# Last projection of a hybrid encoder: weight sums and norm products moved from GpSimd to VectorE

## The chip, the core and the metric

The kernel runs on one core of a Trainium2 chip. A core has TensorE (matrix multiplies, "PE" in the profile, with its weight loads listed apart as "PEld"), VectorE ("DVE"), ScalarE ("ACT"), GpSimd ("POOL"), and SyncE ("SP"), whose queue issues the DMA transfers of this kernel. The engines run side by side, each through its own list of instructions in a fixed order, and wait for each other by semaphores. Matrix multiplies read their operands from the on-chip memory SBUF and add into banks of PSUM; main memory is reached by DMA only. The metric is the device time of one execution in microseconds (us), median of several runs.

## The reference: what is computed

One encoder layer on 1280 tokens (1024 of a prompt, 256 of a sample) with 2048 channels. After an RMS norm and an input projection, eight heads of neighbourhood attention and four heads of a bidirectional mLSTM are computed, gated and put side by side into `mixed`, 2048 channels again. The last step, which this change concerns, is

```python
    mixed = jnp.concatenate([att, mem], axis=-1)
    return x + jnp.einsum('btm,md->btd', mixed, w_out)
# and around it
    x = hybrid_layer(...)
    return rmsnorm(x, final_norm_w)
```

that is, a product of 1280 x 2048 by 2048 x 2048 in fp32, the residual `x`, and a norm over each token's 2048 outputs, multiplied by `final_norm_w`.

## The kernel before

The input projection, the attention and the mLSTM come first and fill the first 2220 us. They are not touched. Their last part, the late gates, runs into the beginning of the last projection.

**The last projection with seven products.** The 2048 output columns are done in two halves, `p = 0` and `p = 1`, of two blocks of 512 columns each (`n0 = 2p`, `n1 = 2p + 1`). `mixed` is cut into four blocks: the tokens in two halves of 640, the 2048 inputs in two halves of 1024. With the weights cut in the same way (B11, B12 the blocks of the first 1024 inputs, B21, B22 those of the last 1024, the second index being the column block), one column half is a 2 x 2 by 2 x 2 block product, and it is done with seven block products in place of eight. `product(p, i, ...)` does the one named `i`, and `operands(p, i, kk)` returns its two operands for one block `kk` of 128 inputs (eight of them). The lists `Aa`, `Ac`, `Ad`, `Ae` hold the blocks of `mixed` in SBUF; `e` is overwritten on the way with sums. The weight operands are

- `i == 2`: B21; `i == 1`: B11; `i == 3`: B22, loaded in pairs of `kk` by `w_pure`;
- `i == 5`: B12 - B11; `i == 6`: `T2`, which is B22 - (B12 - B11); `i == 7`: B22 - B12; `i == 4`: `T2` - B21.

These weight sums are made on chip from blocks of 128 x 512 that `w_block` loads into the buffer pool `po` (six buffers, shared, in turn, by all of them), and, for `T2`, into a slot that held a part of the input `x` before (`xslot`). The order of the products is 2, 5, 1, 6, 7, 4, 3 in the first half and 5, 1, 6, 7, 4, 3, 2 in the second.

**A block of a product.** Both operands are split in two fp32r parts, a rounded one and the rest: `split` (lines 150 to 152) has ScalarE cast (line 151) and VectorE subtract (line 152). The tiles are `mo` (128 x 640, of `mixed`) and `wo` (128 x 512, of the weights), four buffers each. Then TensorE does 15 matmuls of 128x128 by 128x512 (line 1300): three for each of the five token tiles `tt`, into five PSUM banks. The last two blocks of a product are held (`HOLD = 2`) and done bank by bank, so that the banks end one after the other. Then `y_add` (line 1250, VectorE) adds each bank to the output tiles `Y` that it belongs to; where it belongs to two, there are two additions. `Y` starts as the residual, by DMA (`y_init`, line 1257).

**The end of an output tile.** When a tile has got all its additions, `y_done` sums its squares with ScalarE (line 1263), multiplies it with `final_norm_w` (`fnb`) on GpSimd (line 1265) for 30 of the 40 tiles, and stores the tiles of `p = 0` to `yD` in main memory. `finish` reads them back, scales a token's four tiles by the reciprocal root (`rs`, lines 1280 to 1289, two tiny GpSimd instructions each) and stores the result.

**On GpSimd** stand, per block and column half, four weight sums: line 1227 (B12 - B11) and line 1228 (`T2`), both at product 5, line 1241 at product 7 and line 1245 at product 4; and the 30 norm products of line 1265. Other sums of `mixed` blocks (lines 1214, 1231, 1237) are on VectorE.

**Order.** No order is written out by hand here: a scheduler in the compiler orders each engine's instructions by its own estimate of their times, so a change in one place moves others. All DMA transfers of this part are issued from SP's queue, one after the other; a transfer that waits for a buffer holds up those behind it.

Of the kernel before, what the change touches and what calls it, by code (L numbers as in the profile page):

```python
# [11 lines left out]
ALU = mybir.AluOpType  # L12
# [26 lines left out]
def kernel(  # L39
# [17 lines left out]
    V, S, G, PE, DM = nc.vector, nc.scalar, nc.gpsimd, nc.tensor, nc.sync  # L57
# [408 lines left out]
    def po(name):  # L466
        return wb.tile([P, 520], F32, tag="po", name=name, bufs=NPO)

    def w_piece(src, name):
        raw = wb.tile([P, 1024], F32, tag="wraw", name=f"wr_{name}", bufs=2)  # L470
        dst = raw
        if len(src.shape) == 3:
            dst = raw.rearrange("p (j c) -> p j c", j=2)
        DM.dma_start(dst, src)
        return raw
# [699 lines left out]
    def xslot(i, name, dt=F32):  # L1175
        pool, tag = XTAGS[i]
        return pool.tile([P, GB], dt, tag=tag, name=name)
# [10 lines left out]
    fnb = [xslot(28 + i, f"fnb{i}") for i in range(4)]  # L1188
    T2 = {}
    Y = {}  # L1190
# [4 lines left out]
    def w_block(kh, nb, kk, name):  # L1195
        raw = po(f"wb_{name}")[:, :512]
        DM.dma_start(raw, w_o[nb, :, (8 * kh + kk) * 512 : (8 * kh + kk + 1) * 512])
        return raw

    def w_pure(kh, nb, kk, name):  # L1200
        k = 8 * kh + kk
        if kk % 2 == 0:
            src = w_o[nb, :, k * 512 : (k + 2) * 512]
            pair_of["n"] = pair_of.get("n", -1) + 1
            if pair_of["n"] % 3 == 2:
                pair_of["w"] = mp.tile([P, 1024], F32, tag="wr2", name=f"wp_{name}")
                DM.dma_start(pair_of["w"], src)
            else:
                pair_of["w"] = w_piece(src, f"wp_{name}")
        return pair_of["w"][:, (kk % 2) * 512 : (kk % 2 + 1) * 512]  # L1210

    def m_sum(x, y_, op, name):
        t = mp.tile([P, TH], F32, tag="ms", name=name, bufs=2)
        V.tensor_tensor(t, x, y_, op=op)  # L1214
        return t

    def operands(p, i, kk):
        nm = f"{p}_{i}_{kk}"
        n0, n1 = 2 * p, 2 * p + 1
        a, c, d, e = Aa[kk], Ac[kk], Ad[kk], Ae[kk]  # L1220
        if i == 2:
            return d, w_pure(1, n0, kk, nm)
        if i == 5:
            b12, b11 = w_block(0, n1, kk, nm + "a"), w_block(0, n0, kk, nm + "b")
            t = T2[kk] = xslot(20 + kk, f"T2_{nm}")
            DM.dma_start(t, w_o[n1, :, (8 + kk) * 512 : (9 + kk) * 512])
            G.tensor_tensor(b12, b12, b11, op=ALU.subtract)  # L1227
            G.tensor_tensor(t, t, b12, op=ALU.subtract)
            if p:
                return m_sum(e, a, ALU.add, f"ms{nm}"), b12  # L1230
            V.tensor_tensor(e, e, c, op=ALU.add)
            return e, b12
        if i == 1:
            return a, w_pure(0, n0, kk, nm)
        if i == 6:
            if p == 0:
                V.tensor_tensor(e, e, a, op=ALU.subtract)  # L1237
            return e, T2[kk]
        if i == 7:
            b22, b12 = w_block(1, n1, kk, nm + "a"), w_block(0, n1, kk, nm + "b")  # L1240
            G.tensor_tensor(b22, b22, b12, op=ALU.subtract)
            return m_sum(c, e, ALU.subtract, f"ms{nm}"), b22
        if i == 4:
            b21 = w_block(1, n0, kk, nm)
            G.tensor_tensor(b21, T2[kk], b21, op=ALU.subtract)
            return c, b21
        return m_sum(d, e, ALU.subtract, f"ms{nm}"), w_pure(1, n1, kk, nm)

# [10 lines left out]
    def y_done(p, q, tt):  # L1259
        th, nh = divmod(q, 2)  # L1260
        t, c = th * NT + tt, 2 * p + nh
        jk = mp.tile([P, 512], F32, tag="jk", name=f"jk{p}_{q}_{tt}", bufs=1)
        S.activation(jk, Y[p, q, tt], AF.Square, accum_out=ss[t][:, c : c + 1])  # L1263
        if p == 0 or q in (1, 3):
            G.tensor_tensor(Y[p, q, tt], Y[p, q, tt], fnb[c], op=ALU.mult)  # L1265
        if p == 0:
            DM.dma_start(yD[t][:, nh * 512 : (nh + 1) * 512], Y[p, q, tt])

# [25 lines left out]
    def product(p, i, bk, first, each):  # L1294
# [11 lines left out]
        for kk in range(8):  # L1306
            nm = f"{p}_{i}_{kk}"
            ms, wsrc = operands(p, i, kk)
            if tail:
                m = [  # L1310
                    mp.tile([P, TH], F32R, tag=f"mb{z}{z}{kk}", name=f"mo{nm}_{z}") for z in range(2)
                ]
            else:
                t = mp.tile([P, 2, TH], F32R, tag="mo", name=f"mo{nm}", bufs=4)
                m = [t[:, z] for z in range(2)]
            split(*m, ms)
            if tail and kk >= 4:
                w = [xslot(2 * kk + 12 + z, f"wt{nm}_{z}", F32R) for z in range(2)]
            else:
                t = wb.tile([P, 2, 544], F32R, tag="wsp", name=f"wo_{nm}", bufs=4)  # L1320
                w = [t[:, z, :512] for z in range(2)]
            split(*w, wsrc)
            if tail or kk >= 8 - HOLD:
                held.append((kk, m, w))
                continue
            for tt in range(NT):
                mms(tt, kk, m, w, False)
# [13 lines left out]
    for p in range(2):  # L1341

        def reads(bk, *adds, done=None, fin=None):
            def each(tt):
                for q, op in adds:
                    y_add(p, q, tt, bk[tt], op)
                if done is not None:
                    y_done(p, done, tt)
                if fin is not None and p == 1:
                    finish(fin, tt)  # L1350
            return each
# [114 lines left out]
```

## Time and profile before

| | |
|---|---|
| median of 3 runs | 2636.76 us (2635.14 to 2638.74) |
| the profiled execution | 2639.76 us, its span 2637.7 us |
| clock granted to TensorE, mean | 0.996 of full speed |
| first and last weight load of line 1300 | 2222.0 and 2628.1 us |
| GpSimd busy between 2222 and 2629 us | 158.97 us |
| VectorE busy in the same time | 333.56 us |

The profile is of one execution. "Span" runs from its first to its last instruction. A row of a group names the line, the engine, the operation, the tiles written and read, their shapes and the count, then the busy time and the mean length, then the idle time of the engine just before and who ended it (the releaser). Tile names are shortened: `wb_3a` stands for a weight block of `kk = 3`, `T` for `T2`. A row of the time line gives start, length, engine, line, tiles and the number of instructions merged into it. Matmuls overlap, so a row's mean length is longer than the distance between two starts.

### The profile page before, as it was taken

The page shows a single profiled execution, that of the slowest core. Times are in us where ns is not written, and L with a number is a line of the kernel's source. Part 1 is how long each engine was busy: PE and PEld are TensorE (multiplying, and loading weights), DVE is VectorE, ACT ScalarE, POOL GpSimd, SP SyncE. Part 2 cuts the span into 40 slices and gives each one's busy share as a digit, 9 for nine tenths or more (in the row PEclk, how much of TensorE's full clock was granted, in tenths as well). Part 3 has the DMA queues.
Part 4 walks back from the last instruction along what each step waited for, and adds up shares of the span by engine and source line. Part 5 has one row for each costly group of instructions (what it writes and reads, how often), then busy time and mean ns, then how long its engine had stood idle before and what let it go on. Part 6 is the DMA issues. An engine that isn't in the chain of part 4 may idle for free.

```text
span 2637.7 us, 42477 instructions
## 1 busy us (share of the span) xinstructions
PE 2582.4 (98%) x14470; PEld 2364.1 (90%) x14470; DVE 1923.2 (73%) x3744; ACT 1309.2 (50%) x2988; POOL 709.1 (27%) x951
## 2 busy tenths in 40 slices
PE   8999999999999999999999999999999999999998
PEld 8999999999999999988998998989888888787777
DVE  7858778787878778774586587677566644989796
ACT  7534444444444444543565566566566423344435
POOL 0434444444444444300011011010000000436232
PEclk9999999999999999999999999999999999999999
DMA  6423333233333232444655646655554567445327
GB/s 209 150 77 118 107 124 112 95 99 101 95 96 109 77 114 91 163 122 147 193 158 172 198 146 190 201 154 177 186 183 150 178 227 278 158 124 189 103 78 254
DMA packets 215648, 389.10 MB, mean 148 GB/s; under 512 B 26976, under 2 KB 116232, under 8 KB 215432
## 3 DMA queue, kind: packets, MB, share of 16 engines
q1 hardware_dynamic: 215432, 386.40, 46.0%
q8 instruction: 114, 1.87, 0.3%
q14 instruction: 102, 0.84, 0.1%
HBM read 314.94 MB, written 71.38 MB: 146 GB/s over the span
## 4 chain that ended last, share of the span: by engine, by line
PE 45%; DVE 8%; DMA 4%; ACT 2%; issue 1%; SPq 1%; POOL 0%; ACTq 0%; POOLq 0%; DVEq 0%
PE pc L497 21%; PE po L1300 10%; PE pv L578 4%; DVE mo L152 2%; DVE wo L152 1%; PE A54b L188 1%; DMA wr<-in_w_in_dram 1%; DVE ms L1214 1%; PE A52b L188 1%; DVE y L1250 1%; PE nap_0s L615 1%; PE nap_1s L615 1%; DMA nap_0vr<-vD 0%; DVE mb L1237 0%; PE nap_2o L741 0%
## 5 line engine op out<-in xcount | busy, mean ns | idle before, releaser
L1300 PE MATMUL po<-wo,mo 128*128 128x512 f32 x1620 | 381.0, 395 | 12.5 <-DVE wo L152 9.9
L1300 PEld LDWEIGHTS po<-wo,mo 128*128 128x128 f32 x1620 | 303.8, 188 | 88.9 <-DVE wo L152 14.9
L152 DVE TENSOR_TENSOR ws<-wr,ws 128x512 fp32r<-128x512 f32 x224 | 153.3, 695 | 119.3 <-ACT ws L151 118.0
L151 ACT CAST ws<-wr 128x512 fp32r<-128x512 f32 x224 | 136.6, 619 | 179.1 <-PE pc L497 116.8
L151 ACT CAST mo<-mb 128x640 fp32r<-128x640 f32 x72 | 51.8, 725 | 108.1 <-PE po L1300 92.4
L152 DVE TENSOR_TENSOR mo<-mb,mo 128x640 fp32r<-128x640 f32 x72 | 72.9, 1023 | 38.8 <-ACT mo L151 38.8
L1250 DVE TENSOR_TENSOR y<-y,po 128x512 f32<-128x512 f32 x90 | 57.6, 678 | 12.8 <-PE po L1300 12.8
L151 ACT CAST mo<-ms 128x640 fp32r<-128x640 f32 x40 | 29.0, 725 | 70.8 <-PE po L1300 32.5
L102 POOL TENSOR_SCALAR mls_0r<-mls_0r 128x2 f32<-128x2 f32 x4 | 1.2, 289 | 234.0 <-ACT mls_0jk L1087 234.0
L152 DVE TENSOR_TENSOR mo<-ms,mo 128x640 fp32r<-128x640 f32 x40 | 48.5, 1214 | 13.2 <-ACT mo L151 13.2
L1265 POOL TENSOR_TENSOR y<-y,fnb 128x512 f32<-128x512 f32 x30 | 48.1, 1621 | 36.3 <-ACT jk L1263 35.8
L152 DVE TENSOR_TENSOR wsv<-wr_v,wsv 128x512 fp32r<-128x512 f32 x64 | 44.0, 693 | 17.5 <-ACT wsv L151 16.8
L151 ACT CAST wsv<-wr_v 128x512 fp32r<-128x512 f32 x64 | 38.9, 617 | 30.8 <-PE pc L497 19.2
L165 DVE TENSOR_TENSOR pco<-pc,rstdb 128x512 f32<-128x512 f32 x48 | 32.8, 686 | 27.8 <-PE pc L497 26.1
L1227 POOL TENSOR_TENSOR wb_0a<-wb_0a,wb_0b 128x512 f32<-128x512 f32 x2 | 2.6, 1302 | 179.5 <-DMA wb_0b<-in_w_o_dram 179.5
L274 DVE SCALAR_TENSOR_TENSOR pcv<-pco,cw_sb,pcv 128x516 f32<-128x516 f32 x64 | 46.7, 749 | 0.0
L1214 DVE TENSOR_TENSOR ms<-mb,mb 128x640 f32<-128x640 f32 x40 | 45.1, 1127 | 0.0
L1263 ACT ACTIVATE jk<-y 128x512 f32<-128x512 f32 x40 | 25.2, 631 | 39.7 <-DVE y L1250 38.2
L497 PE MATMUL pc<-x_0h,ws 128*128 128x512 f32 x112 | 36.5, 406 | 0.9 <-DVE pco L165 0.9
L497 PE MATMUL pc<-x_2h,ws 128*128 128x512 f32 x112 | 35.3, 399 | 0.0
L188 PE MATMUL fb<-xb,fw 128*128 128x384 f32 x96 | 24.7, 374 | 10.8 <-ACT xb L158 10.8
L188 PE MATMUL fb<-xg,fw 128*128 128x384 f32 x192 | 35.1, 336 | 0.1
(1701 smaller groups left out, 8268.9 us busy)
## 6 DMA issues: line engine op xcount, KB each, us to landing
wr<-in_w_in_dram SPq DMA_DIRECT2D x112, 512.0 KB
wr_v<-in_w_in_dram SPq DMA_DIRECT2D x32, 512.0 KB
xq<-in_xtok_dram SPq DMA_DIRECT2D x20, 512.0 KB
mb<-mx SPq DMA_DIRECT2D x32, 320.0 KB
y<-in_xtok_dram SPq DMA_DIRECT2D x40, 256.0 KB
wr_wp<-in_w_o_dram SPq DMA_DIRECT2D x16, 512.0 KB
xr<-in_xT_dram SPq DMA_DIRECT2D x16, 384.0 KB
nap_0bt<-in_rpb_tab_dram SPq DMA_DIRECT2D x32, 192.0 KB
```

The lines of the kernel that those rows point to most:

```text
L151: S.copy(hi, src)
L152: V.tensor_tensor(lo, src, f(hi), op=ALU.subtract)
L165: V.tensor_tensor(o, src, rb, op=ALU.mult)
L188: PE.matmul(o, w(a_), x(b_), start=first and m == 0, stop=last and m == 2)
L274: V.scalar_tensor_tensor(dst[:, a:n], src[:, a + j - pad : n + j - pad], cw_sb[:, ct, j : j + 1], dst[:, a:n], op0=ALU.mult, op1=ALU.add,)
L497: PE.matmul(pb[j], t[j][:, wi, c : c + P], xs[xi], start=first and m == 0, stop=last and m == 2,)
L578: PE.matmul(outs[tt], xs[:, tt * P : (tt + 1) * P], t[:, wi, q * w : (q + 1) * w], start=first and m == 0 and (gates or tt % 2 == 0), stop ...
L615: PE.matmul(b[:, :nkeys], qs(a_), ks(b_), start=i == 0, stop=i == 2)
L1214: V.tensor_tensor(t, x, y_, op=op)
L1250: V.tensor_tensor(Y[p, q, tt], Y[p, q, tt], bk, op=op)
L1265: G.tensor_tensor(Y[p, q, tt], Y[p, q, tt], fnb[c], op=ALU.mult)
L1300: PE.matmul(bk[tt], m[xi][:, tt * P : (tt + 1) * P], w[wi], start=first and kk == 0 and j == 0, stop=last and j == 2, skip_group_check=True,)
```

## The change

At `i == 5`, B12 is now loaded straight into the slot of `T2` and B11 is subtracted from it there, by VectorE; that tile is product 5's weight operand. At `i == 1`, the next product, B22 is loaded into a `po` buffer and `T2` becomes B22 minus what it held, again by VectorE. The sums of products 7 and 4 and the norm products of `y_done` go from GpSimd (`G`) to VectorE (`V`). The numbers of transfers and matmuls are as before.

```diff
         if i == 5:
-            b12, b11 = w_block(0, n1, kk, nm + "a"), w_block(0, n0, kk, nm + "b")
+            b11 = w_block(0, n0, kk, nm)
             t = T2[kk] = xslot(20 + kk, f"T2_{nm}")
-            DM.dma_start(t, w_o[n1, :, (8 + kk) * 512 : (9 + kk) * 512])
-            G.tensor_tensor(b12, b12, b11, op=ALU.subtract)
-            G.tensor_tensor(t, t, b12, op=ALU.subtract)
+            DM.dma_start(t, w_o[n1, :, kk * 512 : (kk + 1) * 512])
+            V.tensor_tensor(t, t, b11, op=ALU.subtract)
             if p:
-                return m_sum(e, a, ALU.add, f"ms{nm}"), b12
+                return m_sum(e, a, ALU.add, f"ms{nm}"), t
             V.tensor_tensor(e, e, c, op=ALU.add)
-            return e, b12
+            return e, t
         if i == 1:
+            b22 = w_block(1, n1, kk, nm)
+            V.tensor_tensor(T2[kk], b22, T2[kk], op=ALU.subtract)
             return a, w_pure(0, n0, kk, nm)
...
         if i == 7:
             b22, b12 = w_block(1, n1, kk, nm + "a"), w_block(0, n1, kk, nm + "b")
-            G.tensor_tensor(b22, b22, b12, op=ALU.subtract)
+            V.tensor_tensor(b22, b22, b12, op=ALU.subtract)
             return m_sum(c, e, ALU.subtract, f"ms{nm}"), b22
         if i == 4:
             b21 = w_block(1, n0, kk, nm)
-            G.tensor_tensor(b21, T2[kk], b21, op=ALU.subtract)
+            V.tensor_tensor(b21, T2[kk], b21, op=ALU.subtract)
             return c, b21
...
         if p == 0 or q in (1, 3):
-            G.tensor_tensor(Y[p, q, tt], Y[p, q, tt], fnb[c], op=ALU.mult)
+            V.tensor_tensor(Y[p, q, tt], Y[p, q, tt], fnb[c], op=ALU.mult)
```

In the kernel after the change the new sum at `i == 5` is line 1227, that at `i == 1` line 1234, those of products 7 and 4 lines 1242 and 1246, and the norm product line 1266.

## The prediction

> **What bounds the kernel now.** I read the page first, for the whole span, then the time table of stretches for the last projection, then the weight loads of TensorE in order of time, then VectorE and GpSimd beside each other.
>
> ```profile
> span 2637.7 us, 42477 instructions
> PE 2582.4 (98%) x14470; PEld 2364.1 (90%) x14470; DVE 1923.2 (73%) x3744; ACT 1309.2 (50%) x2988; POOL 709.1 (27%) x951
> ```
>
> TensorE is the bound, so the change can only be worth the time in which TensorE stands still in the stage that it touches. That stage is the 1680 matmuls of line 1300; their first and last weight loads:
>
> ```profile
> L1300 PEld LDWEIGHTS po<-wo,mo x1620: 186/188/331, 2222.0 to 2625.4; 128*128 128x128 f32 x180
> L1300 PEld LDWEIGHTS po<-wt,mo x60: 187/188/188, 2607.8 to 2628.1; 128*128 128x128 f32 x60
> ```
>
> From 2222.0 to 2628.3 are 406.3 us. An undisturbed run of the same loads gives the pace (each row: start, length, instructions, idle before it):
>
> ```profile
> 2257.55 3.30 PEld L1300 LDWEIGHTS po<-wo,mo 128*128 128x128 f32 x15 [3.00 <-DVE wo L152]
> ...
> 2292.41 118.12 PEld L1300 LDWEIGHTS po<-wo,mo 128*128 128x128 f32 x512 [0.85 <-issue]
> 2411.68 2.83 PEld L1300 LDWEIGHTS po<-wo,mo 128*128 128x128 f32 x13 [1.15 <-DVE wo L152]
> ...
> 2556.41 51.38 PEld L1300 LDWEIGHTS po<-wo,mo 128*128 128x128 f32 x223 [1.17 <-DVE wo L152]
> ```
>
> 118.12 / 512 is 0.2307 us for a matmul, 3.46 us for a block of 15, 27.7 us for a product of 8 blocks. 1680 x 0.2307 = 387.6, so TensorE loses 406.3 - 387.6 = **18.7 us** in this stage. That is the most that can be won here. It lies almost wholly in two stretches, the product `i == 5` of each column half, and most of it is put down to one cause:
>
> ```profile
> PEld po L1300 <- DVE wo L152: 14.9, 12, 3.0
> ```
>
> ```profile
> 2250.00:2293.00 43.00, 36.71 (x154) 27.95 (x153) 42.97 (x41) 14.82 (x25) 29.92 (x18) 1.00 0.48 152
> 2293.00:2410.00 117.00, 117.00 (x508) 95.11 (x507) 95.61 (x105) 49.64 (x95) 51.86 (x34) 1.00 0.45 139
> 2410.00:2454.00 44.00, 38.50 (x159) 28.72 (x158) 43.57 (x40) 16.84 (x32) 27.31 (x17) 1.00 0.68 215
> ```
>
> Columns: length, then busy time (instructions) of TensorE, its loads, VectorE, ScalarE and GpSimd, the granted clock, DMA share, GB/s. In the first and third stretch VectorE is busy all the time, with only 41 and 40 instructions; in the second it has slack and TensorE has none. So VectorE bounds two short stretches, at about 1.05 us an instruction. Why so slow shows beside GpSimd (minimum/median/maximum in ns, then two stretches of time):
>
> ```profile
> L152 DVE TENSOR_TENSOR mo<-mb,mo x68: 810/824/1931, 2226.6 to 2565.3; 128x640 fp32r<-128x640 f32 x68
> L152 DVE TENSOR_TENSOR wo<-wb,wo x16: 678/680/1786, 2362.9 to 2564.7; 128x512 fp32r<-128x512 f32 x16
> L1250 DVE TENSOR_TENSOR y<-y,po x90: 669/675/689, 2246.4 to 2628.8; 128x512 f32<-128x512 f32 x90
> ```
> ```profile
> 2255.75 1.75 DVE L152 TENSOR_TENSOR wo<-wb_1a,wo 128x512 fp32r<-128x512 f32 x1
> ...
> 2260.71 0.68 DVE L152 TENSOR_TENSOR wo<-wb_2a,wo 128x512 fp32r<-128x512 f32 x1
> ...
> 2285.03 6.05 DVE L1250 TENSOR_TENSOR y<-y,po 128x512 f32<-128x512 f32 x10
> ...
> 2559.09 1.55 DVE L152 TENSOR_TENSOR mo<-mb,mo 128x640 fp32r<-128x640 f32 x2
> ```
> ```profile
> 2239.35 1.31 POOL L1227 TENSOR_TENSOR wb_0a<-wb_0a,wb_0b 128x512 f32<-128x512 f32 x1 [174.98 <-DMA wb_0b<-in_w_o_dram]
> ...
> 2255.11 1.84 POOL L1227 TENSOR_TENSOR wb_3a<-wb_3a,wb_3b 128x512 f32<-128x512 f32 x1
> 2257.02 1.61 POOL L1228 TENSOR_TENSOR T<-T,wb_3a 128x512 f32<-128x512 f32 x1
> 2260.90 1.63 POOL L1227 TENSOR_TENSOR wb_4a<-wb_4a,wb_4b 128x512 f32<-128x512 f32 x1 [2.27 <-DMA wb_5a<-in_w_o_dram]
> ```
>
> The same VectorE instruction takes 0.68 or 1.78 us, and nothing between counts much: a meeting with a GpSimd instruction adds 1.10. The one at 2255.75 meets one, the one at 2260.71 starts while GpSimd waits for a load. The additions out of PSUM (line 1250) never stretch: 689 ns at most.
>
> **The change part by part.** Back to back, VectorE takes (6.05 - 0.68) / 9 = 0.60 us for 512 columns and 1.55 - 0.81 = 0.74 for 640.
>
> *Added to VectorE:* 64 weight sums (four lines, 8 blocks, 2 halves) and the 30 norm products, 94 x 0.60 = **56.4 us**. Nearest row for their price alone: line 152 from wb, 678 ns, same shape and operands in SBUF.
>
> *Removed:* 94 GpSimd instructions, and with them the stretch. Six groups of the stage (busy, mean ns):
>
> ```profile
> L152 DVE TENSOR_TENSOR mo<-mb,mo 128x640 fp32r<-128x640 f32 x68 | 69.8, 1035 | 35.5 <-ACT mo L151 35.5
> L152 DVE TENSOR_TENSOR mo<-ms,mo 128x640 fp32r<-128x640 f32 x40 | 48.5, 1214 | 13.2 <-ACT mo L151 13.2
> L1214 DVE TENSOR_TENSOR ms<-mb,mb 128x640 f32<-128x640 f32 x40 | 45.1, 1127 | 0.0
> ...
> L152 DVE TENSOR_TENSOR wo<-wr_wp,wo 128x512 fp32r<-128x512 f32 x30 | 24.6, 827 | 4.7 <-ACT wo L151 4.7
> ...
> L152 DVE TENSOR_TENSOR wo<-wb,wo 128x512 fp32r<-128x512 f32 x16 | 16.8, 1050 | 0.0
> ...
> L1237 DVE TENSOR_TENSOR mb<-mb,mb 128x640 f32<-128x640 f32 x8 | 11.9, 1485 | 0.1
> ```
>
> Against 0.82 us (640) and 0.68 (512) the excess is 14.0 + 15.7 + 12.3 + 4.2 + 5.9 + 5.3 = **57.4 us**, the smaller groups not counted. VectorE's load therefore does not grow over the stage. The Trainium skill (SBUF — State Buffer, Who interferes with whom) states the same dependence: a VectorE instruction with two SBUF inputs contends with a GpSimd one that reads SBUF, one with at most one SBUF input does not. It says that the loser blocks for the whole instruction of the other; the rows show a fixed 1.10, less than the 1.3 us of a GpSimd sum alone, and by either the cap of 18.7 decides.
>
> *In the two stretches that count:* 41 instructions at 0.60 to 0.74 would be 25 to 30 us in place of 43. Moved in are, in the first half, 8 sums `T - b11`, 8 sums `b22 - T` (the scheduler's order has most of them already among the splits of product 5) and 3 of product 7: 19 x 0.60 = 11.4, so 36 to 42 us. Per block of product 5 that is 0.74 (e + c) + 0.74 + 0.60 (splits) + 2 x 0.60 = 3.28, under TensorE's 3.46. In the second half: 40 instructions, 24 to 30 us; moved in 8 `b22 - T`, 4 of product 7, 5 norm products, 10.2; together 34 to 40, and the 8 `T - b11` fall into product 4 before it, which has room. Product 5 of the first half can begin at 2222.0 + 27.7 = 2249.7 and wants block 2 at 2256.6; walking the new VectorE order with these prices from the last split of product 2 on, that block is ready about 2254, and no later one is late. So both stretches come down to TensorE's own pace: up to 18.7 us gone.
>
> *Moved loads.* Still three loads of 256 KB a block, but the one into T is now B12, on product 5's path; the load of B22 goes into product 1's list, behind the eight b11 loads in SP's queue. T's loads keep their places, all before the first b11, which lands where GpSimd starts today (2239.35), 10 us before product 5 begins. No cost. In SP's queue the stores yD and the loads behind them now wait for VectorE's norm product instead of GpSimd's 1.6 us one: taken as nothing, bound +2 us by the longest stall seen (3.00) less the pace.
>
> *Changed order on TensorE.* The same 1680 matmuls; product 1 now does three banks of three blocks (27 x 0.23 = 6.2 us) before it asks for the last two banks, which VectorE frees 2 to 3 us after product 5's end. No cost by that count.
>
> *New waits.* GpSimd had its own queue to wait for loads; VectorE's is in order, and splits and PSUM additions stand behind each sum. Product 7 is the tight place:
>
> ```profile
> 2344.22 0.33 SPq L1197 DMA_DIRECT2D wb_7b<-in_w_o_dram  x1
> ```
> ```profile
> 2347.24 1.30 POOL L1241 TENSOR_TENSOR wb_7a<-wb_7a,wb_7b 128x512 f32<-128x512 f32 x1 [4.33 <-DMA wb_7b<-in_w_o_dram]
> 2349.19 1.78 POOL L1245 TENSOR_TENSOR wb<-T,wb 128x512 f32<-128x512 f32 x1 [0.66 <-DMA wb<-in_w_o_dram]
> 2351.34 1.46 POOL L1245 TENSOR_TENSOR wb<-T,wb 128x512 f32<-128x512 f32 x1 [0.38 <-DMA wb<-in_w_o_dram]
> ```
> ```profile
> 2341.30 0.69 DVE L1250 TENSOR_TENSOR y<-y,po 128x512 f32<-128x512 f32 x1 [0.70 <-PE po L1300]
> ...
> 2343.51 0.68 DVE L152 TENSOR_TENSOR wo<-wb_2a,wo 128x512 fp32r<-128x512 f32 x1
> ```
>
> A load takes 3.0 us from issue to use and is issued when a split frees a buffer. Product 7 of the first half begins at 2341.3; block 2 is split by 2344.1 and wanted at 2348.2. Going down the new order with 3.0 us a load, 0.60 a sum, the splits stay level with today's (4_0 at 2349.8 instead of 2349.2), but the last sums, 4_6 and 4_7, stand in front of the ten PSUM additions, which then end near 2374.7 with two norm products among them. Product 4 begins at 2341.3 + 27.7 = 2369.0 and wants block 2 at 2375.9; the walk has it at 2376.1. In the second half two early splits of the last product stand there too and one norm product less: + 0.9. New waits: 0.2 + 1.1, with small ones 2.0 us; bounds 0 and 6 (two starts of product 4, each late by one 3.0 us load).
>
> The norm products wait for ScalarE's square of the same tile:
>
> ```profile
> L1263 ACT ACTIVATE jk<-y 128x512 f32<-128x512 f32 x40 | 25.2, 631 | 39.7 <-DVE y L1250 38.2
> ```
>
> In the new order a PSUM addition, a split or a sum stands between an addition and its norm product, 0.6 to 1.3 us against a square of 0.63; what is queued behind are splits two or three blocks (7 to 10 us) ahead of TensorE. No cost; bound 30 x 0.2 = 6 us if each came 0.2 too early and nothing covered it.
>
> *The end* stays: after the last bank there is the same PSUM addition, square, scale and store.
>
> **Sum.** 18.7 - 2.0 = 16.7 us. The profiled execution took 2639.76 (span 2637.7 and 2.06 around it) and would come to 2623.1; it lies 3.0 above the median 2636.76, on which the same gain gives **2620**.
>
> **The rivals.**
>
> *A, slower: VectorE held at the head of its queue by loads.* GpSimd's waits for loads today:
>
> ```profile
> POOL wb L1245 <- DMA wb<-in_w_o_dram: 20.0, 13, 3.4
> ...
> POOL wb_7a L1241 <- DMA wb_7b<-in_w_o_dram: 8.6, 2, 4.3
> POOL wb_6a L1241 <- DMA wb_6b<-in_w_o_dram: 8.0, 2, 4.3
> ```
>
> If buffers come free one by one, a sum costs load 3.0, sum 0.60, cast and split about 1.2: 4.8 us a block instead of 3.46, over the 11 waiting sums of each half (7_5 to 4_7): 22 x 1.34 = 29 us, less 18.7: + 10.8, **2647.5**. It decides from a loop of 3.46 + 18.7 / 22 = 4.3 us. For it: 13 of 16 sums of line 1245 wait. Against: six buffers let loads overlap, and two sums followed each other in 2.15 us today (2349.19, 2351.34). Chance 0.11.
>
> *B, slower: the stretch is not GpSimd's.* Then VectorE, full in both stretches, gets 19 + 17 = 36 more instructions x 0.60 = 21.6 us: **2658**. The Trainium skill speaks for it (Perfetto Trace Analysis, Optimizing Scalar/DVE Operations): when VectorE is saturated, moving work off it, to GpSimd too, may make sense, and this change does the reverse; it adds that moving between those two might not help, as they share a read port. The rows decide for the second half: short whenever GpSimd stands still. Chance 0.03.
>
> *C, half the gain.* The new order makes waits at the starts of products 1, 4 and 6 that my walk, good to a microsecond or two, misses: six of 1.4 us, 8 us, **2628**. Chance 0.14.
>
> *D, it does nothing:* the sums of product 5 arrive late because of their loads, not of VectorE, and B12 now waits for a slot of x. Against it, VectorE has no idle time in these stretches. **2637**, chance 0.06.
>
> **How the numbers follow.** The forecast has 0.66, own range 2616 to 2624. With C that is 0.80, so the range runs from 2614 (all 18.7, and 4 more, as far as the runs shown lie apart) to 2636, where D begins. About 5 us, 0.2%, is what a measurement can tell from no change: faster 0.80, same 0.06, slower 0.11 + 0.03 = 0.14.
>
> **What would show it.** Right: no VectorE instruction of 128x512 or 128x640 over about 0.9 us in the last 400 us; VectorE's busy time in the stage about level; TensorE's loads there idle for 2 to 4 us instead of nearly 20; GpSimd with nothing but the rs pairs. Wrong: VectorE idle before a sum of line 1234, 1242 or 1246 with a load as the releaser, and TensorE waiting for the split behind it; or stretched VectorE instructions without a GpSimd one beside them.

## The result, and the profile after

The changed kernel takes 2621.48 us in the median (2619.05 to 2622.66), the kernel before, beside it, 2637.02 us (2633.03 to 2638.86). The ratio is 0.9944 with a 95% interval from 0.9934 to 0.9955: about 15.5 us, or 0.6%, faster. The forecast was 2620.0.

The profiled execution took 2619.18 us. The first lines of its page (span; busy time, share and instructions of each engine):

```profile
span 2617.5 us, 42412 instructions
PE 2573.3 (98%) x14470; PEld 2361.3 (90%) x14470; DVE 1904.5 (73%) x3838; ACT 1310.7 (50%) x2988; POOL 561.7 (21%) x857
```

VectorE has 94 instructions more than before (3838 against 3744) and is busy 18.7 us less. The weight loads of the last projection, now line 1301:

```profile
L1301 PEld LDWEIGHTS po<-wo,mo x1620: 186/188/191, 2218.3 to 2605.2; 128*128 128x128 f32 x180
L1301 PEld LDWEIGHTS po<-wt,mo x60: 187/188/188, 2589.4 to 2607.9; 128*128 128x128 f32 x60
```

From 2218.3 to 2608.1 (the last load's end) are 389.7 us, 2.1 above the 387.6 of an undisturbed run, where there were 18.7. The stage has got 16.6 us shorter. The profiled executions differ by 2639.76 - 2619.18 = 20.6: 16.6 from the stage, 0.4 from the time around the span, and 3.6 because the stage begins at 2218.3 instead of 2222.0. Nothing ahead of it was changed. Over the twelve profiled executions of this study it begins anywhere from 2216.3 to 2223.9, so below each kernel is judged by the length of this stage, and its median.

The two stretches that TensorE lost time in, in the time table (length, then busy time and instructions of TensorE, its loads, VectorE, ScalarE and GpSimd, granted clock, DMA share, GB/s):

```profile
2250.00:2293.00 43.00, 43.00 (x188) 34.89 (x186) 39.91 (x62) 16.04 (x26) 0.00 (x0) 1.00 0.48 146
...
2410.00:2454.00 44.00, 44.00 (x192) 35.51 (x191) 40.96 (x64) 22.34 (x41) 0.00 (x0) 1.00 0.51 160
```

These are the same stretches of time as in the prediction; the work in them lies a few microseconds further on, since the stage began 3.6 us earlier. TensorE is busy all of the time. VectorE now does 62 and 64 instructions there in place of 41 and 40, in less time. The same groups of VectorE as in the prediction (minimum/median/maximum in ns):

```profile
L152 DVE TENSOR_TENSOR mo<-mb,mo x68: 807/818/826, 2223.0 to 2545.7; 128x640 fp32r<-128x640 f32 x68
...
L152 DVE TENSOR_TENSOR wo<-wb,wo x16: 675/681/684, 2350.2 to 2543.6; 128x512 fp32r<-128x512 f32 x16
...
L1251 DVE TENSOR_TENSOR y<-y,po x90: 670/680/689, 2241.9 to 2608.5; 128x512 f32<-128x512 f32 x90
```

The maxima of the splits were 1931 and 1786 ns and are now 826 and 684; the additions out of PSUM are where they were. Before, 75 VectorE instructions of this stage took more than 0.95 us, and each of them overlaps a GpSimd instruction in the trace; after, none takes that long.

What is left of the loss, in the waits of the stage (who waited, on whom, total us, times, longest):

```profile
PEld po L1301 <- DVE y L1251: 1.3, 1, 1.3
PEld po L1301 <- DVE wo L152: 0.7, 1, 0.7
```
```profile
DVE T L1227 <- DMA wb<-in_w_o_dram: 6.2, 4, 2.1
DVE wb L1246 <- DMA wb<-in_w_o_dram: 5.9, 7, 1.5
...
DVE wb_0a L1242 <- DMA wb_0b<-in_w_o_dram: 3.0, 1, 3.0
```

VectorE does stand still for loads, 15 us of it in these three rows, but TensorE loses only 2.1 in all. Most of that lies late in product 4 and in product 3 of the first half (28.2 and 28.9 us instead of 27.7), where VectorE's time line reads

```profile
2371.86 0.69 DVE L1227 TENSOR_TENSOR T<-T,wb 128x512 f32<-128x512 f32 x1 [1.48 <-DMA wb<-in_w_o_dram]
...
2375.96 0.69 DVE L1227 TENSOR_TENSOR T<-T,wb 128x512 f32<-128x512 f32 x1 [2.07 <-DMA wb<-in_w_o_dram]
...
2381.89 1.36 DVE L1227 TENSOR_TENSOR T<-T,wb 128x512 f32<-128x512 f32 x2 [1.82 <-DMA wb<-in_w_o_dram]
```

These are the sums `T - b11` of the *next* half, put ahead of the splits that product 4 needs now. Their loads come late: in SP's queue they are issued among the stores of the norm products and the residual loads that wait for those stores (31.0 us of waiting in this stage). That this order is what makes them late is read from the rows; no run changed it.

```profile
2366.11 0.39 SPq L1268 DMA_DIRECT2D yD<-y  x1
2366.59 0.38 SPq L1197 DMA_DIRECT2D wb<-in_w_o_dram  x1
2367.02 0.43 SPq L1268 DMA_DIRECT2D yD<-y  x1
2371.13 0.33 SPq L1258 DMA_DIRECT2D y<-in_xtok_dram  x1
2371.55 0.38 SPq L1197 DMA_DIRECT2D wb<-in_w_o_dram  x1
```

### The profile page after: what moved, and what is told of

Same layout as the page of the kernel before. It is cut to its first block, busy times and chain, and to the rows that moved or that the text cites. A ratio compares the mean times of both kernels' runs of the same rounds, so it can differ in the third digit from the quotient of the medians.

```text
span 2617.5 us, 42412 instructions
## 1 busy us (share of the span) xinstructions
PE 2573.3 (98%) x14470; PEld 2361.3 (90%) x14470; DVE 1904.5 (73%) x3838; ACT 1310.7 (50%) x2988; POOL 561.7 (21%) x857
## 4 chain that ended last, share of the span: by engine, by line
PE 51%; DMA 4%; DVE 3%; ACT 1%; issue 1%; SPq 0%; POOL 0%; ACTq 0%; POOLq 0%; DVEq 0%
PE pc L497 22%; PE po L1301 12%; PE pv L578 5%; PE A54b L188 1%; PE A52b L188 1%; DMA wr<-in_w_in_dram 1%; DMA wb<-in_w_o_dram 1%; PE nap_0s L615 1%; PE nap_1s L615 1%; PE nap_2o L741 0%; PE nap_1o L741 0%; PE mlp_2in L919 0%; PE nap_0t L632 0%; PE nap_1t L632 0%; PE nap_0o L741 0%
## 5 line engine op out<-in xcount | busy, mean ns | idle before, releaser
L152 DVE TENSOR_TENSOR mo<-mb,mo 128x640 fp32r<-128x640 f32 x72 | 58.3, 819 | 34.1 <-ACT mo L151 34.1
L152 DVE TENSOR_TENSOR mo<-ms,mo 128x640 fp32r<-128x640 f32 x40 | 32.6, 818 | 7.2 <-ACT mo L151 7.2
L188 PEld LDWEIGHTS fb<-xg,fw 128*128 128x128 f32 x192 | 33.3, 188 | 2.2 <-ACT xg L158 2.2
L497 PE MATMUL pc<-x_2h,ws 128*128 128x512 f32 x112 | 35.2, 399 | 0.0
L497 PE MATMUL pc<-x_1h,ws 128*128 128x512 f32 x112 | 35.2, 404 | 0.0
L497 PE MATMUL pc<-x_8h,ws 128*128 128x512 f32 x112 | 34.8, 398 | 0.0
```

The lines of the kernel that those rows point to most:

```text
L152: V.tensor_tensor(lo, src, f(hi), op=ALU.subtract)
L188: PE.matmul(o, w(a_), x(b_), start=first and m == 0, stop=last and m == 2)
L497: PE.matmul(pb[j], t[j][:, wi, c : c + P], xs[xi], start=first and m == 0, stop=last and m == 2,)
```

## The experiments

"Loss" is the time from the first weight load of the last projection to the end of its last one, less 387.6 us; "products 5" are the lengths of product 5 in the two halves, from its first load to the first of the next product; "long" counts VectorE's additions and subtractions over 0.95 us from 2215 us on; "meeting" below means such a one. Loss, products and long come from one profiled execution each. The two of the changed kernel differ by 1.0 us in the loss, so smaller differences say nothing. The ratio is to the kernel before on the same chip.

| kernel | median us | ratio [95%] | loss | products 5 | long |
|---|---|---|---|---|---|
| before | 2637.02 | 1 | 18.7 | 34.9, 35.2 | 75 |
| changed | 2621.48 | 0.9944 [0.9934, 0.9955] | 2.1 | 27.7, 27.7 | 0 |
| e1: spread, all 94 on GpSimd | 2632.75 | 0.9990 [0.9981, 1.0000] | 14.4 | 34.7, 33.8 | 70 |
| e2: all 94 on VectorE, not spread | 2627.27 | 0.9964 [0.9950, 0.9978] | 7.4 | 29.7, 29.8 | 0 |
| e3: changed + 64 GpSimd additions | 2661.52 | 1.0095 [1.0079, 1.0111] | 42.2 | 35.0, 36.5 | 53 |
| e4: changed + 64 GpSimd fills | 2620.45 | 0.9942 [0.9928, 0.9956] | 1.6 | 27.7, 27.8 | 0 |
| e8: as e3, half the columns | 2634.12 | 0.9998 [0.9989, 1.0007] | 15.4 | 27.7, 28.4 | 41 |
| e5: norm products on GpSimd | 2620.93 | 0.9952 [0.9940, 0.9965] | 2.2 | 27.7, 28.3 | 19 |
| e6: sums of 7 and 4 on GpSimd | 2624.11 | 0.9960 [0.9948, 0.9973] | 3.4 | 27.7, 27.8 | 23 |
| e7: sums of 5 and 1 on GpSimd | 2627.18 | 0.9977 [0.9967, 0.9986] | 9.0 | 33.6, 27.8 | 27 |
| e9: 8 sums on GpSimd | 2618.29 | 0.9930 [0.9917, 0.9944] | 0.3 | 27.7, 27.7 | 7 |
| e10: changed again | 2620.34 | 0.9938 [0.9925, 0.9951] | 1.1 | 27.7, 27.7 | 0 |

Every one of the long instructions of e1 and of e3 to e9 overlaps a GpSimd instruction, as in the kernel before. The reverse does not hold: before, 31 of VectorE's other 199 instructions with two inputs from SBUF overlap one too, for a part or the whole of it, and stay short.

The theory is the prediction's: VectorE instructions with two SBUF inputs stand still while GpSimd reads SBUF, and this costs TensorE time where VectorE has none to spare. The rivals are that the spread of the weight sum, or the loads, made the gain; that GpSimd's own 1.3 to 1.9 us in the chain from load to split was what TensorE waited for; that any work on GpSimd costs; and that a meeting costs the same wherever it lies.

### The two parts apart

The engine put back, the spread kept:

```diff
-            V.tensor_tensor(t, t, b11, op=ALU.subtract)
+            G.tensor_tensor(t, t, b11, op=ALU.subtract)
...
-            V.tensor_tensor(T2[kk], b22, T2[kk], op=ALU.subtract)
+            G.tensor_tensor(T2[kk], b22, T2[kk], op=ALU.subtract)
...
-            V.tensor_tensor(b22, b22, b12, op=ALU.subtract)
+            G.tensor_tensor(b22, b22, b12, op=ALU.subtract)
...
-            V.tensor_tensor(b21, T2[kk], b21, op=ALU.subtract)
+            G.tensor_tensor(b21, T2[kk], b21, op=ALU.subtract)
...
-            V.tensor_tensor(Y[p, q, tt], Y[p, q, tt], fnb[c], op=ALU.mult)
+            G.tensor_tensor(Y[p, q, tt], Y[p, q, tt], fnb[c], op=ALU.mult)
```

> The change's new division of the sums (B12 - B11 in T's slot at product 5, B22 - T at product 1), but all 64 sums and the 30 norm products still on GpSimd. Theory 1 (the gain is the end of the meetings of VectorE and GpSimd instructions that both read two tiles from SBUF): the meetings stay, 60 to 75 VectorE instructions are stretched by 1.10 us, TensorE's loads in the last projection idle 12 us or more, 2630 to 2638 us. Rival 1 (the gain is the spreading: fewer sums ahead of product 5's splits, loads spread over two products): 2619 to 2625 us, stalls gone though instructions are stretched.

Measured: 2632.75 us, 0.999 of the kernel before, at the edge of what can be told from it. The loads and one row of the time table, in the first half's product 5:

```profile
L1301 PEld LDWEIGHTS po<-wo,mo x1620: 186/188/333, 2223.5 to 2622.6; 128*128 128x128 f32 x180
...
L1301 PEld LDWEIGHTS po<-wt,mo x60: 187/188/188, 2605.0 to 2625.3; 128*128 128x128 f32 x60
```
```profile
2252.00:2286.00 34.00, 29.79 (x119) 22.64 (x118) 34.00 (x30) 9.21 (x16) 27.25 (x16) 0.95 0.50 156
```

VectorE is again busy all of the 34 us with 30 instructions, 1.13 us for one. VectorE never stands idle for a sum of GpSimd there, so the chain from load to split is not what holds TensorE. The loss is 14.4: by this execution the spread takes 4.3 of the 18.7 us away by itself. The medians differ by 2.6, with an interval from 0 to 5.

The other part alone is the kernel before with the engine changed:

```diff
-            G.tensor_tensor(b12, b12, b11, op=ALU.subtract)
-            G.tensor_tensor(t, t, b12, op=ALU.subtract)
+            V.tensor_tensor(b12, b12, b11, op=ALU.subtract)
+            V.tensor_tensor(t, t, b12, op=ALU.subtract)
...
-            G.tensor_tensor(b22, b22, b12, op=ALU.subtract)
+            V.tensor_tensor(b22, b22, b12, op=ALU.subtract)
...
-            G.tensor_tensor(b21, T2[kk], b21, op=ALU.subtract)
+            V.tensor_tensor(b21, T2[kk], b21, op=ALU.subtract)
...
-            G.tensor_tensor(Y[p, q, tt], Y[p, q, tt], fnb[c], op=ALU.mult)
+            V.tensor_tensor(Y[p, q, tt], Y[p, q, tt], fnb[c], op=ALU.mult)
```

> The kernel before with the same 94 instructions on VectorE, both sums still at product 5 as before (B12 - B11 into a po buffer, T2 = B22 less that). Theory 1: no stretched VectorE instruction, TensorE's loads idle 2 to 6 us, 2620 to 2626 us. Rival 1 (spreading): 2633 us or more, because product 5 then asks 3.28 us and more of VectorE per block of 3.46 with three loads a block behind it.

Measured: 2627.27 us, loss 7.4, no long instruction; time and loss are a little over what the first theory gave (2626 and 6), and under the rival's 2633. So by this execution the engine alone takes away 11.3 us; 11.3 + 4.3 = 15.6 against 16.6 for both. By the medians it is 8.1 and 2.6 against 15.5. The intervals (6 to 13 us and 0 to 5) allow either, so the shares are known to a few microseconds only; that the engine's is the larger holds in both accounts. What is left, in the time line of the loads (start, length, count, idle before and its releaser) and in that of VectorE:

```profile
2223.91 36.03 PEld L1300 LDWEIGHTS po<-wo,mo 128*128 128x128 f32 x156
2262.12 133.62 PEld L1300 LDWEIGHTS po<-wo,mo 128*128 128x128 f32 x579 [2.18 <-DVE wo L152]
2396.55 3.29 PEld L1300 LDWEIGHTS po<-wo,mo 128*128 128x128 f32 x15 [0.81 <-DVE y L1250]
2400.94 42.38 PEld L1300 LDWEIGHTS po<-wo,mo 128*128 128x128 f32 x184 [1.11 <-ACT jk L1263]
2445.49 12.80 PEld L1300 LDWEIGHTS po<-wo,mo 128*128 128x128 f32 x56 [2.17 <-DVE mo L152]
2459.83 20.16 PEld L1300 LDWEIGHTS po<-wo,mo 128*128 128x128 f32 x88 [1.55 <-issue]
```
```profile
2261.39 0.68 DVE L152 TENSOR_TENSOR wo<-wb_2a,wo 128x512 fp32r<-128x512 f32 x1
...
2439.05 0.69 DVE L1241 TENSOR_TENSOR wb_0a<-wb_0a,wb_0b 128x512 f32<-128x512 f32 x1 [1.86 <-DMA wb_0b<-in_w_o_dram]
...
2444.01 0.69 DVE L1241 TENSOR_TENSOR wb_1a<-wb_1a,wb_1b 128x512 f32<-128x512 f32 x1 [2.19 <-DMA wb_1b<-in_w_o_dram]
```

Each half loses 2 us in product 5. In the first half it waits for the weight split of the third block, at 2261.39, before which VectorE has not paused since 2251; both sums of every block belong to product 5 here. In the second half sums of product 7 (line 1241) stand ahead of product 5's last splits and wait for their loads. Of the 5.3 us between e2 and the changed kernel, how much goes back to the sums and how much to the loads was not separated.

### GpSimd work that reads SBUF, and that does not

The changed kernel, with 64 GpSimd instructions more whose result nobody uses; a one-column instruction ahead of each ties it to the pace of the splits. Once they read (e3), once they only write (e4):

```diff
+    scr = mp.tile([P, 512], F32, tag="scr", name="scr")
...
+            for _ in range({5: 2, 7: 1, 4: 1}.get(i, 0)):
+                G.tensor_tensor(scr[:, :1], f(w[1])[:, :1], f(w[1])[:, :1], op=ALU.add)
+                G.tensor_tensor(scr, fnb[0], fnb[1], op=ALU.add)
```

and in e4 the last line is

```diff
+                G.memset(scr, 0.0)
```

> The changed kernel plus 64 GpSimd additions of two 128x512 tiles from SBUF whose result nobody reads: two behind each block's split of product 5, one behind those of products 7 and 4 (each started by a one-column instruction that waits for the split). VectorE's list keeps its instructions. Theory 1: 45 to 64 VectorE instructions stretched by 1.10 us, VectorE full in the two products 5, 2628 to 2642 us. Rival 2 (the time before was lost because GpSimd's own 1.3 to 1.9 us stood in the chain load - sum - split, not because VectorE was slowed): nobody waits for these additions, 2619 to 2624 us.

> As the run with 64 added GpSimd additions, but each addition is a fill of the same 128x512 tile, which writes SBUF and reads nothing. Theory 1 with the Trainium skill's rule (SBUF - State Buffer, Who interferes with whom: VectorE with two SBUF inputs contends only with a GpSimd instruction that reads SBUF): no VectorE instruction stretched by 1.10 us by a fill, 2619 to 2625 us. Rival 3 (any GpSimd instruction on SBUF stretches VectorE): as with the additions, 2628 us or more.

The order of VectorE's and of TensorE's instructions is the same in both. Measured: 2661.52 us with reads, 2620.45 with fills. The added group and one of the splits, with reads:

```profile
L1327 POOL TENSOR_TENSOR scr<-fnb,fnb x64: 1284/1743/1769, 2242.2 to 2592.6; 128x512 f32<-128x512 f32 x64
...
L152 DVE TENSOR_TENSOR wo<-wb,wo x16: 677/679/1776, 2371.0 to 2584.9; 128x512 fp32r<-128x512 f32 x16
```

and with fills:

```profile
L1327 POOL MEMSET scr<- x64: 525/527/535, 2240.5 to 2548.0; 128x512 f32 x64
...
L152 DVE TENSOR_TENSOR wo<-wb,wo x16: 680/683/715, 2351.2 to 2544.4; 128x512 fp32r<-128x512 f32 x16
```

45 of the 64 fills ran beside a VectorE instruction with two operands in SBUF, and none of these was stretched: the longest took 0.72 us with 512 columns and 0.83 with 640. That any work on GpSimd costs is refuted; reading does. The Trainium skill (SBUF — State Buffer, Who interferes with whom) says this of GpSimd instructions that only write, and the trace agrees.

The time of e3 says less than its single instructions. It lies far above the 2628 to 2642 that the first theory gave, and of the 42.2 us of loss only 16.1 lie in the products 5, while products 1 and 4 lose 20.7. The one-column instructions bring a wait of their own: they read a weight tile `wo`, whose buffer is free for ScalarE's next cast only when GpSimd has got to them. In the waits of e3, of e4 and of e8 (below):

```profile
ACT wo L151 <- POOL scr L1326: 12.6, 9, 3.9
...
ACT wo L151 <- POOL scr L1326: 23.6, 10, 6.1
...
ACT wo L151 <- POOL scr L1326: 28.9, 11, 8.1
```

In e4, 23.6 us of this wait go with a loss of 1.6, so it need not reach TensorE. How the loss of e3 divides between this wait and the stretch was not separated; that the stretch by itself costs TensorE time rests on e1 and on e7 below, which have no such instructions.

### What sets the 1.10 us

The same 64 additions with half the columns, VectorE's and TensorE's instructions in the same order:

```diff
-                G.tensor_tensor(scr, fnb[0], fnb[1], op=ALU.add)
+                G.tensor_tensor(scr[:, :256], fnb[0][:, :256], fnb[1][:, :256], op=ALU.add)
```

> The changed kernel with 64 unused GpSimd additions, as in the kernel with 64 reading additions, but of 128x256 instead of 128x512; every other instruction and its order are the same. Question: what sets the 1.10 us that a meeting costs VectorE? If VectorE is shut out for as long as GpSimd reads, a meeting costs about half: a 128x512 instruction of 0.68 us takes 1.2 to 1.3, and the loss of the stage falls from 42.2 to 10 to 25 us, time 2629 to 2645. If it is a fixed price of a hand-over, the stretched ones still take 1.78 us, the loss is 35 to 45 us and the time 2655 to 2662.

```profile
L1327 POOL TENSOR_TENSOR scr<-fnb,fnb x64: 732/1126/1249, 2242.1 to 2565.5; 128x256 f32<-128x256 f32 x64
...
L152 DVE TENSOR_TENSOR wo<-wb,wo x16: 678/691/1227, 2359.7 to 2559.6; 128x512 fp32r<-128x512 f32 x16
```

The stretched split takes 1227 ns instead of 1776: a meeting costs 0.55 us, half of 1.10. It is no fixed price. GpSimd's own shortest times are 1284 and 732 ns; 256 columns are worth 552 ns, so that 512 are 1104, and 0.18 us go with neither. VectorE is thus held for as long as GpSimd needs for its columns. That this is the time in which GpSimd reads is an inference from the two sizes and from e4.

Loss 15.4 and time 2634.12 lie within what the first theory gave, but not in the place: the products 5 lose 0.7 of it, products 1 lose 8.2, with the wait of ScalarE shown above. In the first half's product 5, which runs at 27.7 us, GpSimd stood still for much of the time. GpSimd, then VectorE:

```profile
2255.50 11.82 POOL L1326 TENSOR_TENSOR scr<-wo 128x1 f32<-128x1 f32 x1 [5.30 <-DVE wo L152]
```
```profile
2266.44 0.82 DVE L152 TENSOR_TENSOR mo<-mb,mo 128x640 fp32r<-128x640 f32 x1
2269.08 0.69 DVE L152 TENSOR_TENSOR wo<-T,wo 128x512 fp32r<-128x512 f32 x1 [1.82 <-ACT wo L151]
```

A one-column addition, 0.19 us at its shortest, takes 11.82. From 2252.60 on VectorE does nothing but instructions with two inputs from SBUF, back to back, and GpSimd's ends at 2267.32, when VectorE's series has ended (2267.26). e4 has the same at 2252.53, for 11.81 us. In e6 below a whole weight sum takes 9.98 us:

```profile
2268.13 9.98 POOL L1242 TENSOR_TENSOR wb_0a<-wb_0a,wb_0b 128x512 f32<-128x512 f32 x1 [204.14 <-DMA wb_0b<-in_w_o_dram]
```
```profile
2276.85 3.69 DVE L1251 TENSOR_TENSOR y<-y,po 128x512 f32<-128x512 f32 x6
```

It ends at 2278.11, 1.26 us after VectorE has turned to additions out of PSUM; 1.28 is the shortest that such a sum takes. So each engine can hold the other, and GpSimd can be held for many VectorE instructions in a row. What decides which of the two waits, the runs don't show.

### Where a meeting costs

The changed kernel with one group at a time back on GpSimd. First the 30 norm products:

```diff
-            V.tensor_tensor(Y[p, q, tt], Y[p, q, tt], fnb[c], op=ALU.mult)
+            G.tensor_tensor(Y[p, q, tt], Y[p, q, tt], fnb[c], op=ALU.mult)
```

> The changed kernel with the 30 norm products back on GpSimd. Question: does every meeting of a GpSimd product with a VectorE instruction cost TensorE time, or only one where VectorE has none to spare? Theory 1 (only where VectorE is full, that is product 5 of each half): most of the norm products run beside products 1, 4, 3 and 2, where VectorE has slack; only the handful at the start of product 5 of the second half (the first half's last tiles) can be felt: loss of the stage 3 to 6 us against 2.1 in the changed kernel, time 2621 to 2626. Theory 2 (each meeting costs its 1.10 us wherever it lies): up to 30 x 1.10 = 33 us, 2640 to 2655.

Then the 32 sums of products 7 and 4:

```diff
-            V.tensor_tensor(b22, b22, b12, op=ALU.subtract)
+            G.tensor_tensor(b22, b22, b12, op=ALU.subtract)
...
-            V.tensor_tensor(b21, T2[kk], b21, op=ALU.subtract)
+            G.tensor_tensor(b21, T2[kk], b21, op=ALU.subtract)
```

> The changed kernel with the 32 sums of products 7 and 4 back on GpSimd. Theory 1: about as many meetings as there are sums, but none in product 5, so hardly any of it reaches TensorE; and the sums that wait for a load no longer stand in VectorE's queue: loss of the stage under 4 us (2.1 in the changed kernel), time 2619 to 2624, at best a microsecond or two under the changed kernel. Theory 2: 32 x 1.10 = 35 us or, with the meetings half as many, 18 us more: 2638 to 2656.

And the 32 of products 5 and 1:

```diff
-            V.tensor_tensor(t, t, b11, op=ALU.subtract)
+            G.tensor_tensor(t, t, b11, op=ALU.subtract)
...
-            V.tensor_tensor(T2[kk], b22, T2[kk], op=ALU.subtract)
+            G.tensor_tensor(T2[kk], b22, T2[kk], op=ALU.subtract)
```

> The changed kernel with the 32 sums of products 5 and 1 back on GpSimd: as many as in the kernel that gives back those of 7 and 4, but these are the ones that run while VectorE is full. Theory 1: most of the loss of the kernel with all 94 back (14.4 us) returns: 10 to 14 us, in the two products 5 (32 to 35 us each in place of 27.7), time 2628 to 2634. Theory 2: the same as with the sums of products 7 and 4.

The norm products make 19 meetings, some 19 x 1.10 = 21 us of VectorE's time, and TensorE loses 2.2 us, no more than in the changed kernel (3 to 6 were expected, and 2621 to 2626 for the time, which is 2620.93). The sums of 7 and 4 make 23 meetings and a loss of 3.4 (under 4 was expected), at 2624.11, where up to 2624 was given. Most of that loss is one place, which is no meeting (e6, loads, then VectorE):

```profile
2329.92 52.12 PEld L1301 LDWEIGHTS po<-wo,mo 128*128 128x128 f32 x226
2384.42 0.30 PEld L1301 LDWEIGHTS po<-wo,mo 128*128 128x128 f32 x2 [2.38 <-issue]
```
```profile
2374.47 0.69 DVE L1227 TENSOR_TENSOR T<-T,wb 128x512 f32<-128x512 f32 x1 [3.48 <-DMA wb<-in_w_o_dram]
...
2382.88 0.69 DVE L1227 TENSOR_TENSOR T<-T,wb 128x512 f32<-128x512 f32 x1 [2.49 <-DMA wb<-in_w_o_dram]
```

It is the wait of `T - b11` again that the changed kernel has. The sums of 5 and 1 make 27 meetings, hardly more, but 13 of them lie in the stretch in which VectorE works for the first half's product 5, and that product takes 33.6 us:

```profile
2234.97 24.29 PEld L1301 LDWEIGHTS po<-wo,mo 128*128 128x128 f32 x105
2260.41 0.30 PEld L1301 LDWEIGHTS po<-wo,mo 128*128 128x128 f32 x2 [1.16 <-ACT mo L151]
...
2271.24 0.30 PEld L1301 LDWEIGHTS po<-wo,mo 128*128 128x128 f32 x2 [2.84 <-issue]
```

In all the loss is 9.0 (10 to 14 were expected) and the time 2627.18 (2628 to 2634 were). The intervals of the ratios of e6 and e7 overlap; it is the traces that set them apart. That a meeting costs the same wherever it lies is refuted by e5 and e6 (2640 to 2656 were its numbers).

The second half's product 5 stays near 27.7 us in each of the three (28.3, 27.8, 27.8), and takes 33.8 in e1, where all are on GpSimd. While TensorE is in that product, 3, 2 and 5 instructions are long in the three, and 14 in e1. So the groups' losses don't add up. That VectorE's slack covers a few meetings there and not fourteen fits these counts; it was not tested by itself.

### The rest of the loss

The changed kernel with the eight sums `T - b11` of the second half alone on GpSimd, so that no load is waited for at the head of VectorE's queue:

```diff
-            V.tensor_tensor(t, t, b11, op=ALU.subtract)
+            (G if p else V).tensor_tensor(t, t, b11, op=ALU.subtract)
```

> The changed kernel with only the eight sums of product 5 of the second half (line 1227) on GpSimd; TensorE's order is the same, VectorE's too but for these eight and a few neighbours. Question: are the last 2.1 us that TensorE loses due to these sums standing at the head of VectorE's queue while their loads are on the way? If so: VectorE no longer idles for a load between 2365 and 2385, products 4 and 3 of the first half run at 27.7 us in place of 28.2 and 28.9, the loss of the stage is 0.5 to 1 us, though up to eight meetings come back (8 x 1.10 us, at a place where VectorE idled 6 us); time 1 to 2 us under the changed kernel, within what can be told. If the lost time belongs to the norm products or to the splits themselves, the loss stays at 2 us or, with the meetings, grows to 4 to 8.

Its partner is the changed kernel, unchanged:

> The changed kernel once more, on the same chip as the kernel with eight sums on GpSimd, as its partner: 2619 to 2623, loss of the stage 1.5 to 2.5 us.

In e9's loads the place where products 4 and 3 lost time is one run without a gap:

```profile
2349.94 70.14 PEld L1301 LDWEIGHTS po<-wo,mo 128*128 128x128 f32 x304
```
```profile
L1301 PEld LDWEIGHTS po<-wo,mo x1620: 186/188/190, 2216.9 to 2601.9; 128*128 128x128 f32 x180
...
L1301 PEld LDWEIGHTS po<-wt,mo x60: 187/188/188, 2586.1 to 2604.6; 128*128 128x128 f32 x60
```

The loss is 0.3 us, though seven meetings have come back. The changed kernel beside it loses 1.1, in product 3 (28.5 us), less than the 1.5 to 2.5 that were expected. The medians are 2618.29 and 2620.34; their intervals overlap, so that e9 is faster than the changed kernel isn't shown by the times. What its trace shows is that TensorE loses next to nothing in this stage once VectorE doesn't wait for these loads.

## Why the prediction was right, and where it was not

**The bound and the cap: right.** All that moved between the kernels is the loss of TensorE in this stage, 18.7 us before. 16.7 were forecast to go and 16.6 went; the medians differ by 15.5. That the two agree to 0.1 us is luck: the changed kernel's second execution loses 1.1 in place of 2.1, and the 2.0 that the sum takes off stands for other waits than those that came (below).

**The cause, "a meeting with a GpSimd instruction adds 1.10": right in size, wrong in kind.** No long instruction is left without GpSimd's reads, and they come back with them (e1, e3). But the prediction read 1.10 as fixed, since a GpSimd sum alone takes 1.3 us. e8 shows that it goes with the columns that GpSimd reads. The rule of the Trainium skill (SBUF — State Buffer, Who interferes with whom), that the loser is blocked for the whole instruction of the other, was nearer than the reading of the rows: 1.10 of 1.28 us and 0.55 of 0.73, all but 0.18 us in both. The prediction counted only what VectorE loses; that GpSimd is held too, for up to 11.8 us, it did not have.

**Added 56.4, removed 57.4, VectorE's load "about level": the second term too small.** VectorE is busy 313.6 us in the changed kernel's stage against 333.3, so that with 56.4 added some 76 were taken away. The prediction counted six groups and left out the small ones; by its own rule all groups together have 76 us over 0.68 and 0.82 an instruction. It changed no forecast, as the two stretches were counted apart: 36 to 42 us for 60 instructions and 34 to 40 for 57 were given for VectorE there, and 39.91 for 62 and 40.96 for 64 measured.

**"Moved loads ... No cost" and the spread: a part that was given no price.** The prediction's sum is for the whole change, and its text puts the gain down to the end of the stretch alone. By the execution of e2 the engine alone is worth 11.3 us, and without the spread 7.4 stay lost, 2 of them in product 5 of each half. The sum came out right because both parts were made at once.

**New waits of 2.0 us: the size right, the place wrong.** Expected were the last sums of product 4 ahead of ten PSUM additions, late by 0.2 and 1.1. Measured is a loss of 2.1 in one execution and 1.1 in the other, by the sums `T - b11` of the next half. Of these the prediction said that they "fall into product 4 before it, which has room". Their time has room; their loads were not asked after. And the stores and residual loads in SP's queue, "taken as nothing, bound + 2 us", stand ahead of just these loads. e9, in which that wait is taken from VectorE, loses 0.3. So the 2 us bound of that term held, and its middle value of nothing did not.

**The rivals.** A, VectorE held by loads in products 7 and 4, did not come: VectorE waits for loads there, 5.9 and about 4.6 us in all, and TensorE runs on, because splits are ready ahead. B, by which the stretch was not GpSimd's, is refuted by the result itself, in which no instruction is stretched, and by e1 and e8. The Trainium skill (Perfetto Trace Analysis, Optimizing Scalar/DVE Operations) says that moving work off a saturated VectorE, to GpSimd too, may make sense, and that between these two it might not help. Here it costs: e1 has the 94 instructions on GpSimd and takes 2632.75. C's six waits at the starts of products 1, 4 and 6 did not come: these take 27.7 to 27.9 us in the changed kernel, but for the 28.2 of the first half's product 4. D is refuted by the result.

## What to carry to other kernels

Where a VectorE instruction with both inputs in SBUF has two lengths and nothing between, look what GpSimd reads at that time: in these runs one was held by the other where the two met, and a 128x512 sum that VectorE does in 0.60 us could take 1.10 from it on GpSimd. But count only the meetings in stretches where VectorE is full and the bounding engine waits for it; the 19 of e5, most of them elsewhere, cost nothing that shows. When a test adds instructions to an engine, look which buffers they hold, as the one-column ones of e3 and e8 did. When work goes onto an in-order queue, ask of each moved instruction where its load stands in the DMA queue, not only whether its engine has time; fills, and the few sums that would wait for a load, may stay on GpSimd.

## What the runs showed of the hardware that was not expected

- A meeting's price goes with the columns that GpSimd reads: 1.10 us at 512 (e3), 0.55 at 256 (e8).
- GpSimd pays as well: its median is 1743 ns against a shortest of 1284 at 512 columns (e3), and 1126 against 732 at 256 (e8). Beside VectorE instructions with two SBUF inputs back to back, a one-column addition was held for 11.8 us (e4, e8) and a 128x512 one for 9.98 (e6).
- GpSimd fills of 128x512 (527 ns each) stretched no VectorE instruction (e4).
- The same, untouched first 2220 us end up to 7.6 us apart from one execution to the next, half of what this change is worth.
